# The low parts of the output projections' weights by an accumulating DMA in place of VectorE

## The chip, the cores and the metric

The kernel runs on one core of one Trainium2 chip. The metric is the device time of one execution in microseconds, as the median of several runs. The kernel before takes 1111.75 us (3 runs, 1111.43 to 1113.39).

## The reference

A trunk of two decoder layers over 512 tokens of width 1024, all in float32. Layer a mixes by causal pooling, layer b by stick-breaking attention against a shared K/V; both have four memory attention heads beside the mixer, an output projection and a SwiGLU feed-forward part. The change concerns the output projections alone (`a_w_out` and `b_w_out` below):

```python
def pool_layer(x, mem, mem_norm, norm_mix, w_in, w_group, scale, w_mem_kv, w_out, norm_ffn, w_gu, w_down):
    ...
    x = x + jnp.concatenate([grouped, mem_out], axis=-1) @ w_out
    return x + swiglu(rmsnorm(x, norm_ffn), w_gu, w_down)

def sb_layer(x, mem, k_sh, v_sh, mem_norm, norm_mix, w_q, w_mem_kv, w_out, norm_ffn, w_gu, w_down):
    ...
    x = x + jnp.concatenate([sb_out, mem_out], axis=-1) @ w_out
    return x + swiglu(rmsnorm(x, norm_ffn), w_gu, w_down)
```

## The kernel before, in words

TensorE multiplies in a reduced float32 form (fp32r), so each operand is split in a high part (the value rounded to fp32r) and a low part (the rest). `mm3` (L252 to L259) forms a product in three matmuls: wh·xh (L257), wh·xl (L258) and wl·xh (L259); the low part of the weight is thus needed by the third.

The weights come in bricks of 128 x 512. `bricks` (L169) walks the list PLAN of all bricks; SyncE (SP) loads two bricks per DMA of 512 KB (L183) into one of NRAW = 4 raw chunks `wr_...`, and `wsplit` (L198) makes of each brick `wh` (a cast by ScalarE, ACT, L209) and `wl` (a subtraction by VectorE, DVE, L210, or L213 and L214 where a gain belongs to the weight). There are 4 buffers of wh and 4 of wl, and `next_brick` makes bricks AHEAD = 2 before the one in use. A brick of an output projection feeds 12 matmuls of TensorE (PE): 4 output tiles, three matmuls each. A raw chunk is free for the next load when both its bricks are split, and a wl buffer when the last third matmul of its brick has read it.

The projections a_out and b_out have 16 bricks each, called here b0 to b15. Their matmuls are woven into the attention heads by two blocks in which the order on PE is written out from a planner's estimates (`chain`, `wait`); elsewhere, and on all other engines, a scheduler orders the instructions. On the way: SP also issues the copies of the keys `kh<-hk` and `kb<-kl` (L518), that the scores `zs` (L589, L590) read; ACT makes the softmax terms of memory attention (`pt`, L571 and L576), transposed by PE (`tp`, L540); GpSimd (POOL) masks (`nb`, `be`, L594 and L596) and adds up squares for the next norm (`ssq`, L270). `evac` adds the projection to the residual stream on DVE (`x`, L742).

Of the kernel before, what the change touches and what calls it, by code (L numbers as in the profile page):

```python
# [11 lines left out]
F32 = mybir.dt.float32  # L12
F32R = mybir.dt.float32r
AF = mybir.ActivationFunctionType
ALU = mybir.AluOpType
# [98 lines left out]
class Net:  # L114
# [50 lines left out]
    def bricks(self):  # L165

        at, chunk = {}, {}
        for name, ks, gains in PLAN:
            w = self.a[name]  # L169
            _, _, cb, cols = w.shape  # L170
            for k in ks:
                i = at.get(name, 0)
                at[name] = i + 1
                c, b = divmod(i, cb)
                if b == 0:
                    t = self.wp.tile([P, cb, cols], F32, tag="wraw", name=f"wr_{name}_{c}", bufs=NRAW)
                    if i == 0 and name == "a_in":
                        for j in range(cb):
                            self.nc.sync.dma_start(t[:, j, :], w[c, :, j, :])
                            if j == 0:  # L180
                                self.first()
                    else:
                        self.nc.sync.dma_start(t, w[c])  # L183
                    chunk[name] = t
                yield name, self.wsplit(chunk[name][:, b, :], k, gains, name == "b_last")

    def next_brick(self, name):

# [6 lines left out]
        assert got == name  # L195
        return parts

    def wsplit(self, w, k, gains=None, stays=False):  # L198

        nc = self.nc  # L200
        cols = w.shape[-1]
        self.chain([("act", cols), ("dve", cols)])
        if stays:
            wh, wl = self.t("xh", F32R), self.t("xl", F32R)
        else:
            wh = self.wp.tile([P, cols], F32R, tag="wh", name="wh", bufs=4)
            wl = self.wp.tile([P, cols], F32R, tag="wl", name="wl", bufs=4)
        if gains is None:
            nc.scalar.copy(wh, w)  # L209
            nc.vector.tensor_tensor(out=wl, in0=w, in1=wh.bitcast(F32), op=ALU.subtract)  # L210
        else:
            for c0, c1, g in gains:
                nc.scalar.activation(wh[:, c0:c1], w[:, c0:c1], AF.Copy, scale=self.gain(g, k))  # L213
                nc.vector.scalar_tensor_tensor(  # L214
                    out=wl[:, c0:c1], in0=w[:, c0:c1], scalar=self.gain(g, k),
                    in1=wh.bitcast(F32)[:, c0:c1], op0=ALU.mult, op1=ALU.subtract)
        return wh, wl
# [792 lines left out]
def _chunks(bricks, cb=2):  # L1010
    b = np.stack(bricks)
    n, p, c = b.shape
    return np.ascontiguousarray(b.reshape(n // cb, cb, p, c).transpose(0, 2, 1, 3))
# [63 lines left out]
```

## Time and profile before

| | |
|---|---|
| median of 3 runs | 1111.75 us |
| the profiled execution | 1111.37 us, of which the span of the profile 1109.7 us |
| PE, PEld busy | 1086.1 us (98%), 912.8 us (82%) |
| DVE, ACT, POOL busy | 677.1 us (61%), 499.8 us (45%), 79.1 us (7%) |
| granted TensorE clock, mean | 0.996 |
| DMA | 117.48 MB, 106 GB/s in the mean; none is issued by POOL |

The times in the rows are microseconds from the span's start. A matmul's own duration is longer than its distance to the next, because matmuls overlap: the distance says what one costs. What stands in brackets at a row's end is how long the engine had been idle ahead of it, and what ended that. The projection a_out lies between 88 and 146 us, b_out between 654 and 737 us.

### The profile page before, as it was taken

To read this page: it belongs to the slowest core of one execution; us is meant where nothing else is said; L and a number is where in the kernel's file an instruction comes from. 1 tells how busy PE (TensorE), PEld (TensorE's weight loads), DVE (VectorE), ACT (ScalarE), POOL (GpSimd) and SP (SyncE) were. 2 spreads that over 40 slices of the span, in tenths; PEclk is the share of its full clock that TensorE was granted. 3 is DMA by queue.
4 is the path that set the end of the run, shared out by engine and by line. 5 is a ranking of instruction groups with operands and counts; after the bars stand their busy time and mean duration, and the time that the engine had idled before them with its cause. 6 is when DMAs were issued, how large, how long until landed. Compare 5 with 4: busy or idle time off the path is not lost.

```text
span 1109.7 us, 14396 instructions
## 1 busy us (share of the span) xinstructions
PE 1086.1 (98%) x5280; PEld 912.8 (82%) x5280; DVE 677.1 (61%) x1118; ACT 499.8 (45%) x913; POOL 79.1 (7%) x126
## 2 busy tenths in 40 slices
PE   9989999999999999999999999999999999999997
PEld 7988888888888888888877887788888888888887
DVE  7987666543454534565579698884563365435574
ACT  7558444332333323344797576553332233323343
POOL 0000120000000000000013143240000000000000
PEclk9999999999999999999999999999999999999999
DMA  7454222322222222323445424122222223222212
GB/s 272 138 175 124 95 90 93 102 96 95 95 95 95 95 97 102 103 96 92 138 133 131 132 84 111 60 93 95 95 96 99 97 100 103 96 95 95 95 57 77
DMA packets 39366, 117.48 MB, mean 106 GB/s; under 512 B 5120, under 2 KB 7168, under 8 KB 39296
## 3 DMA queue, kind: packets, MB, share of 16 engines
q1 hardware_dynamic: 39152, 116.54, 32.5%
q8 instruction: 41, 0.67, 0.2%
q14 instruction: 29, 0.24, 0.1%
q10 hardware_dynamic: 144, 0.03, 0.0%
HBM read 100.83 MB, written 2.10 MB: 93 GB/s over the span
## 4 chain that ended last, share of the span: by engine, by line
PE 53%; issue 40%; DVE 3%; ACT 2%; DMA 1%; POOL 1%; SPq 0%; POOLq 0%; DVEq 0%; ACTq 0%
PE acc L257 15%; PE acc L258 15%; PE acc L259 15%; PE av L629 2%; PE tp L540 1%; DVE wl L214 1%; DVE it L599 1%; DMA wr_a_in<-in_a_in_dram 1%; PE zs L590 0%; DMA kb<-kl 0%; PE last L257 0%; PE zs L589 0%; PE last L258 0%; PE last L259 0%; POOL nb L594 0%
## 5 line engine op out<-in xcount | busy, mean ns | idle before, releaser
L257 PE MATMUL acc<-xh,wh 128*128 128x512 f32 x880 | 342.9, 392 | 2.1 <-DVE mx L567 1.1
L258 PE MATMUL acc<-xl,wh 128*128 128x512 f32 x880 | 342.8, 390 | 0.0
L259 PE MATMUL acc<-xh,wl 128*128 128x512 f32 x880 | 342.1, 390 | 0.0
L257 PEld LDWEIGHTS acc<-xh,wh 128*128 128x128 f32 x880 | 165.2, 188 | 35.4 <-ACT xh L223 1.7
L259 PEld LDWEIGHTS acc<-xh,wl 128*128 128x128 f32 x880 | 165.2, 188 | 34.7
L258 PEld LDWEIGHTS acc<-xl,wh 128*128 128x128 f32 x880 | 165.4, 188 | 32.9 <-DVE xl L224 0.2
L214 DVE SCALAR_TENSOR_TENSOR wl<-wr_a_gu,gains,wh 128x512 fp32r<-128x512 f32 x88 | 67.0, 762 | 110.8 <-ACT wh L213 110.8
L214 DVE SCALAR_TENSOR_TENSOR wl<-wr_b_gu,gains,wh 128x512 fp32r<-128x512 f32 x88 | 66.9, 762 | 105.5 <-ACT wh L213 105.5
L213 ACT ACTIVATE wh<-wr_a_gu,gains 128x512 fp32r<-128x512 f32 x88 | 63.6, 724 | 139.0 <-PE acc L258 111.8
L257 PE MATMUL acc<-hh,wh 128*128 128x512 f32 x320 | 124.5, 389 | 0.0
L258 PE MATMUL acc<-hl,wh 128*128 128x512 f32 x320 | 124.5, 389 | 0.0
L259 PE MATMUL acc<-hh,wl 128*128 128x512 f32 x320 | 124.3, 389 | 0.0
L213 ACT ACTIVATE wh<-wr_b_gu,gains 128x512 fp32r<-128x512 f32 x88 | 63.6, 724 | 133.4 <-PE acc L258 104.0
L258 PEld LDWEIGHTS acc<-hl,wh 128*128 128x128 f32 x320 | 60.1, 188 | 12.5
L259 PEld LDWEIGHTS acc<-hh,wl 128*128 128x128 f32 x320 | 60.1, 188 | 12.5
L257 PEld LDWEIGHTS acc<-hh,wh 128*128 128x128 f32 x320 | 60.1, 188 | 12.4
L210 DVE TENSOR_TENSOR wl<-wr_a_down,wh 128x512 fp32r<-128x512 f32 x44 | 30.4, 690 | 60.1 <-ACT wh L209 49.9
L286 POOL TENSOR_TENSOR rs<-var,mhalf 128x4 f32<-128x4 f32 (+1 forms) x7 | 6.6, 942 | 758.3 <-DVE var L284 758.3
L209 ACT CAST wh<-wr_a_down 128x512 fp32r<-128x512 f32 x44 | 27.4, 622 | 72.6 <-PE acc L258 67.9
L210 DVE TENSOR_TENSOR wl<-wr_b_down,wh 128x512 fp32r<-128x512 f32 x36 | 24.8, 690 | 49.1 <-ACT wh L209 41.0
L257 PE MATMUL acc<-mixh,wh 128*128 128x512 f32 x128 | 51.0, 399 | 0.3 <-DVE x L742 0.3
L259 PE MATMUL acc<-mixh,wl 128*128 128x512 f32 x128 | 50.2, 392 | 0.0
(199 smaller groups left out, 1696.7 us busy)
## 6 DMA issues: line engine op xcount, KB each, us to landing
wr_a_gu<-in_a_gu_dram SPq DMA_DIRECT2D x44, 512.0 KB, 3.4
wr_b_gu<-in_b_gu_dram SPq DMA_DIRECT2D x44, 512.0 KB, 3.4
wr_a_down<-in_a_down_dram SPq DMA_DIRECT2D x22, 512.0 KB, 3.4
wr_b_qkv<-in_b_qkv_dram SPq DMA_DIRECT2D x20, 512.0 KB, 3.6
wr_b_down<-in_b_down_dram SPq DMA_DIRECT2D x18, 512.0 KB, 3.4
wr_a_out<-in_a_out_dram SPq DMA_DIRECT2D x8, 512.0 KB, 3.5
wr_b_out<-in_b_out_dram SPq DMA_DIRECT2D x8, 512.0 KB, 3.4
wr_a_in<-in_a_in_dram SPq DMA_DIRECT2D x7, 512.0 KB, 4.2
```

What stands on the lines that cost most here:

```text
L209: nc.scalar.copy(wh, w)
L210: nc.vector.tensor_tensor(out=wl, in0=w, in1=wh.bitcast(F32), op=ALU.subtract)
L213: nc.scalar.activation(wh[:, c0:c1], w[:, c0:c1], AF.Copy, scale=self.gain(g, k))
L214: nc.vector.scalar_tensor_tensor(out=wl[:, c0:c1], in0=w[:, c0:c1], scalar=self.gain(g, k), in1=wh.bitcast(F32)[:, c0:c1], op0=ALU.mult, o ...
L257: mm(ps, wh, xh, start=first, stop=False)
L258: mm(ps, wh, xl, start=False, stop=False)
L259: mm(ps, wl, xh, start=False, stop=last)
L286: nc.gpsimd.tensor_tensor(out=rs, in0=var, in1=self.mhalf[:, :nt], op=ALU.pow)
L540: nc.tensor.transpose(tp[:, i * P:(i + 1) * P], blk, self.ident)
L599: nc.vector.tensor_tensor_scan(out=it[:, :end][:, ::-1], data0=nb[:, :end][:, ::-1], data1=nb[:, :end][:, ::-1], initial=1.0, op0=ALU.mult ...
L629: self.nc.tensor.matmul(to, vv, part, start=ia == 0 and i == 0, stop=ia == nu - 1 and i == len(parts) - 1)
```

## The change

For the bricks of a_out and b_out the low part is no longer a DVE subtraction. ACT writes the negated high part into wl (an added pass over 128 x 512), and POOL issues a DMA of 256 KB that adds the raw weight to what stands in wl. All other bricks are as before.

```diff
@@ bricks @@
-                yield name, self.wsplit(chunk[name][:, b, :], k, gains, name == "b_last")
+                yield name, self.wsplit(chunk[name][:, b, :], k, gains, name == "b_last", name.endswith("_out"))
@@ wsplit @@
-    def wsplit(self, w, k, gains=None, stays=False):
+    def wsplit(self, w, k, gains=None, stays=False, dma=False):
...
         if gains is None:
             nc.scalar.copy(wh, w)
-            nc.vector.tensor_tensor(out=wl, in0=w, in1=wh.bitcast(F32), op=ALU.subtract)
+            if dma:
+                nc.scalar.activation(wl, wh.bitcast(F32), AF.Copy, scale=-1.0)
+                nc.gpsimd.dma_start(wl.bitcast(F32), w, accum_op=ALU.add)
+            else:
+                nc.vector.tensor_tensor(out=wl, in0=w, in1=wh.bitcast(F32), op=ALU.subtract)
```

The lines below the edit move down by four (L540 becomes L544, and so on); the added pass is L211, the DMA L212. The planner's list of work is the same, so the order on PE inside the two blocks is the same. DVE loses 32 instructions, ACT gains 32, POOL 32 DMAs. Where the scheduler decides, it moves some. Three places follow.

ACT at the start of a_out, where the heads of memory attention end. `wh_1174` is the high part of b0 and `wr_a_out_0`, `_1` the raw chunks of b0 to b3. Before:

```order
L551 COPY tb_1138<-av_1117 64x512
L223 CAST ath_1146<-tp_1141 128x512
L571 ACTIVATE pt_1120,sm_1129<-zm_1121,mx_1126,sp_324 128x256 x2
L209 CAST wh_1206<-wr_a_out_0_1172 128x512
L223 CAST ath_1155<-tp_1150 128x512
L814 ACTIVATE mixh_1181<-accg_1159,gains_67 128x512
L576 ACTIVATE pt_1120<-pt_1120,sm_1129 128x256 x2
L209 CAST wh_1233<-wr_a_out_1_1231 128x512
L814 ACTIVATE mixh_1213<-accg_1160,gains_67 128x512
L209 CAST wh_1297<-wr_a_out_1_1231 128x512
L571 ACTIVATE pt_1188,sm_1197<-zm_1189,mx_1194,sp_324 128x256 x2
L814 ACTIVATE mixh_1220<-accg_1161,gains_67 128x512
```

And now, from the negation of b1 on (`pt_1189`, `mixh_1215` and `mixh_1222` were `pt_1188`, `mixh_1213` and `mixh_1220`):

```order
L211 ACTIVATE wl_1208<-wh_1207 128x512
L580 ACTIVATE pt_1120<-pt_1120,sm_1129 128x256 x2
L575 ACTIVATE pt_1189,sm_1198<-zm_1190,mx_1195,sp_324 128x256 x2
L209 CAST wh_1300<-wr_a_out_1_1233 128x512
L818 ACTIVATE mixh_1215<-accg_1160,gains_67 128x512
L211 ACTIVATE wl_1236<-wh_1235 128x512
L555 COPY tb_1245<-av_1226 64x512
L580 ACTIVATE pt_1189<-pt_1189,sm_1198 128x256 x2
L575 ACTIVATE pt_1252,sm_1261<-zm_1253,mx_1258,sp_324 128x256 x2
L211 ACTIVATE wl_1301<-wh_1300 128x512
L818 ACTIVATE mixh_1222<-accg_1161,gains_67 128x512
```

The negations of b1 and b2 (`wl_1208`, `wl_1236`) stand ahead of the normalisation of `pt_1189`, as does that of b0, which stands right behind the cast of `ath_1146`; one `mixh` pass has moved behind it.

SP where b_out begins: `wr_b_out_4` (buffer `wr_b_out_6854` here) goes into the raw chunk of b0 and b1 of b_out. Before:

```order
L183 DMA wr_b_out_6830<-in_b_out_dram 128x1024 [waits DMAHW2_49,DVE_49]
L518 DMA kh<-hk 64x512 [waits DMAHW3_49,Activation_49]
L518 DMA kh<-hk 64x512 [waits DMAHW4_49]
L518 DMA kh<-hk 64x512 [waits DMAHW5_49]
L518 DMA kh<-hk 64x512 [waits DMAHW6_49]
L518 DMA kb<-kl 64x512 [waits DMAHW7_49,DVE_49]
L518 DMA kb<-kl 64x512 [waits DMAHW0_49]
```

And now:

```order
L183 DMA wr_b_out_6854<-in_b_out_dram 128x1024 [waits DMASW1_49,DMAHW2_49,DMASW0_49,Activation_49]
L522 DMA kh<-hk 64x512 [waits DMAHW3_49,Activation_49]
L522 DMA kh<-hk 64x512 [waits DMAHW4_49]
L522 DMA kh<-hk 64x512 [waits DMAHW5_49]
L522 DMA kb<-kl 64x512 [waits DMAHW6_49,DVE_49]
L522 DMA kb<-kl 64x512 [waits DMAHW7_49]
L522 DMA kh<-hk 64x512 [waits DMAHW0_49]
```

The load waited for DVE and now waits for the two accumulating DMAs of b0 and b1 (DMASW0 and DMASW1); the copies of the keys stand behind it, and one `kh` has changed places with the first two `kb`. The DMA of b1 stands on POOL behind the select of `be` that ran at 660.25.

POOL at the end of a_out. Before, all rows of a_out:

```order
L286 TENSOR_TENSOR rs_473<-var_471,mhalf_76 128x2
L270 TENSOR_TENSOR ssq_1452<-ssq_1452,sq_1467 128x512
L270 TENSOR_TENSOR ssq_1452<-ssq_1452,sq_1483 128x512
L270 TENSOR_TENSOR ssq_1452<-ssq_1452,sq_1499 128x512
L270 TENSOR_TENSOR ssq_1452<-ssq_1452,sq_1631 128x512
```

Now, from the tenth DMA on (`wr_a_out_5` holds b10 and b11):

```order
L212 DMA wl_1448<-wr_a_out_4_1437 128x512
L274 TENSOR_TENSOR ssq_1462<-ssq_1462,sq_1477 128x512
L212 DMA wl_1519<-wr_a_out_5_1516 128x512
L212 DMA wl_1536<-wr_a_out_5_1516 128x512
L274 TENSOR_TENSOR ssq_1462<-ssq_1462,sq_1493 128x512
L274 TENSOR_TENSOR ssq_1462<-ssq_1462,sq_1509 128x512
L212 DMA wl_1555<-wr_a_out_6_1552 128x512
L212 DMA wl_1572<-wr_a_out_6_1552 128x512
L212 DMA wl_1591<-wr_a_out_7_1588 128x512
L212 DMA wl_1608<-wr_a_out_7_1588 128x512
L274 TENSOR_TENSOR ssq_1462<-ssq_1462,sq_1647 128x512
```

The DMAs of b10 and b11 stand behind the first addition of squares, those of b12 to b15 behind the third. At the end of both projections PE has also moved: behind the first two matmuls of b15 stand matmuls of the feed-forward part (18 in layer b, 6 in layer a) ahead of the first that reads the wl of b15.

## Rows read from the trace of the kernel before

**Rows 1.** The page's first part: busy time of each engine over the span.
```profile
PE 1086.1 (98%) x5280; PEld 912.8 (82%) x5280; DVE 677.1 (61%) x1118; ACT 499.8 (45%) x913; POOL 79.1 (7%) x126
```

**Rows 2.** Windows: from:to, length, busy us of each engine, PE clock, DMA share, GB/s.
```profile
95.00:105.00 10.00, 9.12 (x47) 7.38 (x47) 7.75 (x17) 9.95 (x26) 0.00 (x0) 1.00 0.31 106
...
680.00:695.00 15.00, 15.00 (x77) 12.29 (x76) 14.73 (x25) 10.65 (x25) 7.88 (x15) 1.00 0.10 36
```

**Rows 3.** Waits of PE over the whole span: us in total, times, longest.
```profile
PE tp L540 <- ACT pt L576: 3.0, 3, 1.2
PE zs L590 <- DMA kb<-kl: 2.8, 2, 1.8
```

**Rows 4.** Lines L209 and L210: duration in ns (minimum/median/maximum), first and last start.
```profile
L209 ACT CAST wh<-wr_a_out x16: 602/622/638, 88.6 to 134.4; 128x512 fp32r<-128x512 f32 x16
...
L210 DVE TENSOR_TENSOR wl<-wr_a_out,wh x16: 679/691/1772, 89.3 to 135.1; 128x512 fp32r<-128x512 f32 x16
```

**Rows 5.** DMA issues: times issued, KB each, median us from issue to landing.
```profile
wr_a_out<-in_a_out_dram SPq DMA_DIRECT2D x8, 512.0 KB, 3.5
...
kh<-hk SPq DMA_DIRECT2D x24, 128.0 KB, 2.4
...
xin<-in_x_dram SPq DMA_DIRECT2D x8, 256.0 KB, 6.8
```

**Rows 6.** Timeline of POOL: start, us, instruction, times, idle before.
```profile
123.69 1.68 POOL L270 TENSOR_TENSOR ssq<-ssq,sq 128x512 f32<-128x512 f32 x1 [86.36 <-ACT sq L266]
...
660.25 0.93 POOL L596 TENSOR_SCALAR_AFFINE_SELECT be<-be 128x128 f32<-128x128 f32 x1
...
699.44 2.54 POOL L594 TENSOR_SCALAR_AFFINE_SELECT nb<-nb 128x128 f32<-128x128 f32 x1 [0.38 <-ACT nb L592]
701.93 0.29 POOL L596 TENSOR_SCALAR_AFFINE_SELECT be<-be 128x128 f32<-128x128 f32 x1
```

**Rows 7.** Timeline of ACT in a_out.
```profile
90.83 0.59 ACT L223 CAST ath<-tp 128x512 fp32r<-128x512 f32 x1
91.31 0.57 ACT L571 ACTIVATE pt<-zm,mx,sp 128x256 f32<-128x256 f32 x1
...
98.69 0.91 ACT L576 ACTIVATE pt<-pt,sm 128x256 f32<-128x256 f32 x2
...
123.52 1.12 ACT L209 CAST wh<-wr_a_out 128x512 fp32r<-128x512 f32 x2
```

**Rows 8.** Timeline of PE in a_out.
```profile
95.73 0.39 PE L259 MATMUL acc<-mixh,wl 128*128 128x512 f32 x1
...
99.25 0.72 PE L540 MATMUL tp<-ident,pt 128*128 128x128 f32 x2 [0.81 <-ACT pt L576]
...
129.41 0.39 PE L259 MATMUL acc<-mixh,wl 128*128 128x512 f32 x1
129.64 0.39 PE L257 MATMUL acc<-mixh,wh 128*128 128x512 f32 x1
```

**Rows 9.** Timeline of SP where b_out begins: the issues themselves.
```profile
659.98 0.33 SPq L183 DMA_DIRECT2D wr_b_out<-in_b_out_dram  x1
664.28 2.39 SPq L518 DMA_DIRECT2D kh<-hk  x4
667.01 2.39 SPq L518 DMA_DIRECT2D kb<-kl  x4
```

**Rows 10.** Timeline of PE where b_out begins, and at 729.
```profile
669.90 0.33 PE L590 MATMUL zs<-kb,qs 128*128 128x128 f32 x1 [1.81 <-DMA kb<-kl]
...
729.22 0.39 PE L259 MATMUL acc<-mixh,wl 128*128 128x512 f32 x1
729.90 0.50 PE L257 MATMUL acc<-mixh,wh 128*128 128x512 f32 x1 [0.29 <-DVE x L742]
```

**Rows 11.** Windows around the wait of 668: columns as in rows 2.
```profile
671.10:674.50 3.40, 3.40 (x17) 3.20 (x16) 1.68 (x4) 1.17 (x2) 0.21 (x1) 0.51 0.55 125
```

**Rows 12.** Timeline of DVE at the end of b_out.
```profile
727.45 1.79 DVE L210 TENSOR_TENSOR wl<-wr_b_out,wh 128x512 fp32r<-128x512 f32 x1
```

## The prediction

> **What bounds the kernel now.** I read the busy times first: PE is busy for 98% of the span, DVE for 61%, POOL for 7% [rows 1]. Work taken from DVE is therefore worth something only where PE waits for DVE. The windows tell where that could be [rows 2]: between 680 and 695 DVE is busy for 14.73 of 15 us, but PE for all 15.00, so a faster DVE brings nothing there; between 95 and 105 it is ACT that is full (9.95 of 10), and PE misses 0.88. The list of waits names what ends these gaps [rows 3]: ACT's `pt`, and the copy of the keys `kb`; neither names a low part of a weight. The timelines give the places: 0.81 ahead of `tp` at 99.25 [rows 8], 1.81 ahead of `zs` at 669.90, and 0.29 ahead of the projection's first matmul at 729.90 [rows 10]. Of the three only the last is behind DVE's `wl`: that subtraction took 1.79 at 727.45 where its median is 0.69 [rows 4, 12], the residual add came after it, and PE waited for the add.
>
> **What is removed and added.** 32 subtractions of 0.69 leave DVE: 22 us of an engine with 433 us to spare. ACT gets 32 passes of 128 x 512. I price one as the cast of the same size: 0.62 by itself [rows 4], 0.50 when it follows another, since two casts back to back took 1.12 [rows 7]; 16 to 20 us in all. PE's matmuls are the same in number. So the engine sums decide nothing; what decides is how long the new low part takes to be there, and who stands behind it. Call L the time from POOL's issue of the accumulating DMA to wl landed. Before, the step between wh and the use was a subtraction of 0.69; now it is a pass on ACT and L.
>
> **The size of L.** No row shows an accumulate, nor any DMA that POOL issues. The nearest rows: a plain copy of 128 KB takes 2.4 from issue to landing, a load of 512 KB 3.5, the slowest landing of a 256 KB tile (at the kernel's start) is 6.8 [rows 5]. The accumulate moves 256 KB but reads two operands, 512 KB; by bytes it is nearest to the 3.5. POOL must also write the list of transfers itself; the nearest rows for a pass of POOL are 0.93 (a select) and 1.68 (an add) [rows 6], 1.3 in the middle. I take L = 3.5 + 1.3 = 4.8, with 2.4 and 6.8 as ends. The lower end could only undercut a plain copy of half the bytes, which I exclude.
>
> The copy of 128 KB here takes 2.4 and the load of 512 KB 3.5 [rows 5]. The Trainium skill (DMA: Bandwidth & Descriptors, section "Anatomy of one DMA — SWDGE (gpsimd) path") gives about 2.0 us plus the bytes over 436 KB per us for a DMA issued by GpSimd, and both rows lie close to that line. By it 256 KB would take an estimated 2.6, and the sum below would be that of the first rival.
>
> **First term: the start of a_out.** The first matmul that reads a low part of a_out is at 95.73 [rows 8]. The negation of b0 now stands behind the cast of `ath` (90.83), where a `pt` pass began at 91.31; it ends at 91.31 + 0.62 = 91.93 [rows 7]. The budget is 95.73 - 91.93 = 3.80, and with L = 4.8 PE waits 1.0. There is a second path: ACT is full here, three negations come ahead of the `pt` normalisation at 98.69 that ended the wait of 0.81, and one pass leaves: net two of 0.50, another 1.0 on that wait. The two overlap, because a PE that is 1.0 late anyway asks for `tp` 1.0 later. The term is the larger: max(1.0, L - 3.80) = +1.0. Below zero it can't go, since nothing leaves ACT here. Bricks b1 to b9 cost nothing at that L; the cover is the two bricks that are prepared ahead, 5.4 us of PE, since a brick is 12 matmuls and they start 0.23 apart (129.41, 129.64) [rows 8].
>
> **Second term: b10.** At the end of a_out the DMAs stand on POOL between additions of squares. The casts of b10 and b11 start at 123.52 and 124.02, the negation of b10 at 124.52 and ends at 125.14 [rows 7]; POOL is in its addition until 123.69 + 1.68 = 125.37 [rows 6]; the low part is wanted at 129.41 [rows 8]. Budget 4.04, cost L - 4.04 = +0.76. From then on PE is later by that much and the bricks behind it, with the same two bricks of cover less the passes of ACT, are inside it. Without the additions in the way the budget would be 4.27, so the queue itself costs 0.23. The last brick of each layer is covered by the matmuls of the feed-forward part that now stand ahead of it (6 x 0.23 = 1.4 in a, 18 x 0.23 = 4.1 in b); without this cover b15 of layer b, issued only behind two additions of 1.68 on POOL, would cost up to 3.4.
>
> **Third term: SP at the start of b_out.** The load of the fifth raw chunk must wait until both DMAs on the first chunk have read it, and the copies of the keys are queued behind it on SP. The DMA of b1 leaves POOL behind the select that ends at 660.25 + 0.93 = 661.18 [rows 6]; it lands at 665.98; the load's issue takes 0.33, so the first `kh` goes at 666.31 in place of 664.28 [rows 9]. With 0.60 for each issue (2.39 for four) three `kh` and the first `kb` are through at 668.71, and the second `kb` issues there. Before, it issued at 667.01 + 0.60 = 667.61, and `zs` ran 2.29 later, at 669.90 [rows 10]. Now it runs at 671.00: the wait of 1.81 grows by 1.10, or L - 3.70. Waiting behind `zs` on PE is all the rest of b_out. The selects of POOL, which stand behind its DMAs, are the other thing that moves; PE is full from 680 on [rows 2], so I cost them at nothing; the cover is the projection's own matmuls, woven between the heads, and if it is gone each DMA's 1.3 on POOL is a price that the first heads would pay.
>
> **What is gained.** Without the subtraction at 727.45 the residual add comes as soon as PE is done with its tile, and the matmul at 729.90 follows 0.23 after that of 729.22, as others do: 0.45 less [rows 10, 12]. What is late next is nothing on that chain.
>
> **The sum.** 1.0 + 0.76 + 1.10 - 0.45 = +2.4 in the profiled execution of 1111.37 us (span 1109.7, 1.67 around it). That execution is 0.38 below the median of the runs, 1111.75, and the difference is put onto the median: 1114.2. The bounds: at L = 2.4 only the ACT path is left, 1.0 - 0.45 = +0.55; at L = 6.8 it is 3.0 + 2.76 + 3.10 - 0.45 = +8.4.
>
> **Rivals.** *The DMA lands in time.* L at most 3.7: +0.55, 1112.3, no measurable change (a measurement of this kernel tells 0.2%, 2.2 us). For it speak the plain copies at 2.4, against it the doubled reads. The sum passes 2.2 at L = 4.7, so this is the rival on the other side of the line: not slower for every L below that.
>
> *The clock follows the wait.* Right behind the wait of 1.81 the granted clock was 0.51 for 3.4 us [rows 11], the level of 1.2 GHz, which cost 1.7. The wait at 99.25, now 0.81 with no drop behind it in a window at 1.00 [rows 2], would become 1.8 if the ACT path and not b0 sets it. A second drop makes 1115.9.
>
> *POOL is held up while it writes.* A select of the same shape took 2.54 at 699.44 and 0.29 at 701.93, beside DVE work [rows 6]. If a DMA's list is stretched by that difference, 2.25, L is 7.05 and the sum 3.25 + 3.01 + 3.35 - 0.45 = +9.2: 1120.9. Against it: DVE is emptier now. The Trainium skill (SBUF — State Buffer, section "Who interferes with whom") has a DVE instruction with two inputs contend only with a GpSimd instruction that reads SBUF; by that rule the writing of the list would be spared, and L would stay near 4.8.
>
> *DVE's relief reaches the keys.* With L under 2.8 SP isn't held, `kl` can come up to a subtraction (0.69) earlier, and if the shorter wait also spares the clock drop (1.7), the sum is 0 (ACT absorbed) - 0.45 - 0.69 - 1.7 = -2.8: 1108.9. It needs three things at once.
>
> **Chances.** The forecast case (L from 4.1 to 5.6, its own range 1112.7 to 1116.6) has 0.40, in time 0.29, the clock 0.11, POOL held up 0.13, the keys 0.07. Of the forecast case some two thirds lie above the line of 2.2: slower 0.27 + 0.11 + 0.13 = 0.51, same 0.29 + 0.13 = 0.42, faster 0.07. The range leaves out the far part of POOL's rival and most of the keys': 1111.2 to 1119.5.
>
> **What would show it.** The rows of the DMA on POOL give L itself. Right if PE's list has waits on it near 96 and 130, a longer wait for `kb` near 670, and none for the add at 729. Wrong if PE between 95 and 146 waits no more than before (L small), if PE waits show between 680 and 725 (POOL's selects late), or if more than 4 us of waits stand at other bricks, which would mean that two bricks ahead do not cover L.

## The result, and the profile after

The changed kernel takes 1121.45 us (median of 4 runs, 1120.59 to 1122.42) against 1111.64 before (4 runs): a ratio of 1.0089, with a 95% interval from 1.0077 to 1.0101. It is slower by 9.8 us, where +2.4 was forecast and 1119.5 was the upper end. The profiled execution has a span of 1118.9 us, 9.2 more than before. The engine sums moved about as worked out, against [rows 1]: DVE lost 19.5 us, ACT gained 19.0, POOL 26.0, and PE's busy time grew by 3.8 us at the same number of matmuls, of which 2.5 is time at a low clock (table below). The first part of the page:

```profile
PE 1089.9 (97%) x5280; PEld 913.9 (82%) x5280; DVE 657.6 (59%) x1086; ACT 518.8 (46%) x945; POOL 105.1 (9%) x158
```

The DMA issues of the page (times issued, KB each, median us from issue to landing) give the size that no row of before had. L is 3.7 and 3.2 in the median, not 4.8, and POOL is busy for 0.87 per DMA. The copies of the keys have become slower, 3.0 and 2.8 where they took 2.4 [rows 5] and 2.5:

```profile
wl<-wr_a_out POOLq DMA_DIRECT2D x16, 256.0 KB, 3.7
...
wl<-wr_b_out POOLq DMA_DIRECT2D x16, 256.0 KB, 3.2
...
kh<-hk SPq DMA_DIRECT2D x24, 128.0 KB, 3.0
kb<-kl SPq DMA_DIRECT2D x24, 128.0 KB, 2.8
```

So the transfer is quicker than forecast and the kernel slower. PE's list of waits (us in total, times, longest) says where to look. Against [rows 3], `tp` has grown by 0.9, and three lines are new: `kh`, `mixl`, and the low part itself, which has only 1.0 of it:

```profile
PE tp L544 <- ACT pt L580: 3.9, 3, 1.7
...
PE zs L593 <- DMA kh<-hk: 2.4, 1, 2.4
PE zs L594 <- DMA kb<-kl: 2.4, 2, 1.3
PE acc L261 <- DVE mixl L819: 2.1, 1, 2.1
...
PE acc L263 <- DMA wl<-wr_a_out: 1.0, 1, 1.0
```

**Lining up the matmuls.** PE's order is the same in both kernels through most of the two projections, so each matmul of one execution can be set against the same matmul of the other, and the difference of their starts read as a running delay. This is the table that it gives (us from each span's start):

| PE instruction | before | after | delay | what came since the line above |
|---|---|---|---|---|
| `av`, before the first wait | 95.96 | 95.91 | -0.05 | |
| `tp` | 99.25 | 100.10 | +0.85 | wait for `pt`, 1.70 in place of 0.81: +0.9 |
| a_out, the next tile | 100.52 | 103.61 | +3.09 | wait for `mixl`, 2.08: +2.2 |
| a_out | 103.27 | 108.89 | +5.62 | half clock: +2.5 |
| a_out, b12's low part used | 134.85 | 141.66 | +6.81 | wait for the DMA, 1.00: +1.2 |
| `zs` of the keys before b_out | 631.42 | 638.79 | +7.37 | +0.6, in many small pieces |
| `zs<-kb` | 669.90 | 679.46 | +9.56 | `kh` 2.44 and `kb` 1.33 in place of 1.81: +2.2 |
| b_out, behind the add | 729.90 | 738.97 | +9.07 | the wait of 0.29 is gone: -0.5 |

**The start of a_out.** On ACT (timeline: start, us, instruction) the negation of b2 stands at 98.37 ahead of the `pt` normalisation, which comes at 99.54 where it came at 98.69 [rows 7]; the third `mixh` pass is now behind the negation of b3, at 102.09. DVE makes `mixl` of it at 102.80, and PE's next matmul waits for that until 103.61. It then takes 0.79 and its followers 0.63, where such a matmul takes 0.39:

```profile
98.37 0.66 ACT L211 ACTIVATE wl<-wh 128x512 fp32r<-128x512 f32 x1
99.05 0.58 ACT L555 COPY tb<-av 64x512 f32<-64x512 f32 x1
99.54 0.91 ACT L580 ACTIVATE pt<-pt,sm 128x256 f32<-128x256 f32 x2
...
101.57 0.62 ACT L211 ACTIVATE wl<-wh 128x512 fp32r<-128x512 f32 x1
102.09 0.68 ACT L818 ACTIVATE mixh<-accg,gains 128x512 fp32r<-128x512 f32 x1
```

The same pass before, the `mixl` that DVE makes of it, and PE's matmul, which waited for neither:

```profile
97.46 0.72 ACT L814 ACTIVATE mixh<-accg,gains 128x512 fp32r<-128x512 f32 x1
```

```profile
98.94 0.74 DVE L815 SCALAR_TENSOR_TENSOR mixl<-accg,gains,mixh 128x512 fp32r<-128x512 f32 x1
```

```profile
100.52 0.39 PE L257 MATMUL acc<-mixh,wh 128*128 128x512 f32 x1
```

DVE's row now, and below it three of PE's:

```profile
102.80 0.75 DVE L819 SCALAR_TENSOR_TENSOR mixl<-accg,gains,mixh 128x512 fp32r<-128x512 f32 x1 [0.93 <-ACT mixh L818]
```

```profile
100.10 0.73 PE L544 MATMUL tp<-ident,pt 128*128 128x128 f32 x2 [1.70 <-ACT pt L580]
...
103.61 0.79 PE L261 MATMUL acc<-mixh,wh 128*128 128x512 f32 x1 [2.08 <-DVE mixl L819]
104.20 0.63 PE L262 MATMUL acc<-mixl,wh 128*128 128x512 f32 x1
```

The windows (columns as in rows 2) show the two costs apart: from 95 to 105 PE is busy for 6.15 where it was 9.12 [rows 2], and from 105 to 115 it is full, but at a granted clock of 0.80: part of that stretch ran at the level of 1.2 GHz, where before it was 1.00 throughout.

```profile
95.00:105.00 10.00, 6.15 (x28) 4.45 (x27) 5.08 (x12) 9.95 (x26) 2.62 (x3) 0.86 0.61 128
105.00:115.00 10.00, 10.00 (x42) 8.09 (x40) 1.45 (x3) 5.58 (x11) 2.37 (x3) 0.80 0.46 109
```

And the second of these stretches before:

```profile
105.00:115.00 10.00, 10.00 (x50) 8.26 (x49) 4.71 (x8) 4.51 (x9) 0.00 (x0) 1.00 0.22 69
```

**The end of a_out.** The DMA of b12 leaves POOL at 135.54, behind the additions of squares, and PE wants it at 140.66. That is 5.1 later, more than the usual L; but this one takes 6.1:

```profile
141.66 0.50 PE L263 MATMUL acc<-mixh,wl 128*128 128x512 f32 x1 [1.00 <-DMA wl<-wr_a_out]
```

The view of line L212 in a window around a single DMA (issues with durations in ns, then the time to landing) shows two sizes: 3.2 for the one at 111.63, with no load and no other accumulating DMA under way, and 6.1 for the one at 135.54, right beside the load that SP issues at 135.88. A load is let go as soon as the accumulating DMAs on its raw chunk have landed (the later of b10's and b11's at 135.7), so the two kinds meet again and again. Of the 16 DMAs of a_out the five that left within 0.7 of a load (99.32, 114.37, 122.95, 135.54 and 136.3) took 4.5 to 6.6. A sixth slow one, 5.3 from 138.88, left while two others were still under way. The other ten took 3.2 to 4.0.

```profile
L212 POOL DMA_DIRECT2D wl<-wr_a_out x1: 872/872/872, 111.6 to 111.6; - x1
...
DMA to landing us min/median/max: 3.2/3.2/3.2
```

```profile
L212 POOL DMA_DIRECT2D wl<-wr_a_out x1: 879/879/879, 135.5 to 135.5; - x1
...
DMA to landing us min/median/max: 6.1/6.1/6.1
```

And SP's issue of the load in its timeline:

```profile
135.88 0.33 SPq L183 DMA_DIRECT2D wr_a_gu<-in_a_gu_dram  x1
```

The Trainium skill's line for a DMA issued by GpSimd (DMA: Bandwidth & Descriptors, "Anatomy of one DMA — SWDGE (gpsimd) path") makes an estimated 2.6 of 256 KB. An accumulate alone took 3.2 here, so that line is nearer than the 4.8 of the forecast, and it does not tell of the 6.1.

**The start of b_out.** SP's load of the fifth raw chunk went out at 672.2, and the copies of the keys follow it at 672.59. Taken back by the delay of 7.37 that is 665.22, 0.94 later than in [rows 9]. Each copy then lands in 4.2 to 4.6 us; the copies of before landed in 2.2 to 2.3 there. PE waits 2.44 for `kh`, which it did not wait for at all before, and 1.33 for `kb`. The late issue alone would have cost little: before, the second `kb` was issued at 667.51 and `zs` ran 2.39 later; now it is issued at 675.05, which plus 2.39 is 677.44, or 670.07 by the time of before, an estimated 0.2 more than 669.90. The other 2.0 are the slow landing. SP's timeline first:

```profile
658.26 14.24 SPq L183 DMA_DIRECT2D wr_b_out<-in_b_out_dram  x2
672.59 1.75 SPq L522 DMA_DIRECT2D kh<-hk  x3
674.55 1.10 SPq L522 DMA_DIRECT2D kb<-kl  x2
```

The landing of the copies issued between 672 and 676 (line L522), that of the six of before (line L518, 664 to 668), and PE's two waits now:

```profile
DMA to landing us min/median/max: 4.2/4.4/4.6
```

```profile
DMA to landing us min/median/max: 2.2/2.3/2.3
```

```profile
677.83 0.30 PE L593 MATMUL zs<-kh,qs 128*128 128x128 f32 x1 [2.44 <-DMA kh<-hk]
679.46 0.45 PE L594 MATMUL zs<-kb,qs 128*128 128x128 f32 x1 [1.33 <-DMA kb<-kl]
```

### The profile page after: what moved, and what is told of

Same layout as the page of the kernel before. It is cut to its first block, busy times and chain, and to the rows that moved or that the text cites. A ratio compares the mean times of both kernels' runs of the same rounds, so it can differ in the third digit from the quotient of the medians.

```text
span 1118.9 us, 14469 instructions
## 1 busy us (share of the span) xinstructions
PE 1089.9 (97%) x5280; PEld 913.9 (82%) x5280; DVE 657.6 (59%) x1086; ACT 518.8 (46%) x945; POOL 105.1 (9%) x158
## 4 chain that ended last, share of the span: by engine, by line
PE 87%; DVE 4%; ACT 3%; issue 2%; DMA 2%; POOL 1%; SPq 0%; POOLq 0%; DVEq 0%; ACTq 0%
PE acc L261 27%; PE acc L263 27%; PE acc L262 26%; PE av L633 2%; PE tp L544 1%; DMA kb<-kl 1%; DVE wl L218 1%; PE zs L594 1%; DMA wl<-wr_a_out 1%; DMA wr_a_in<-in_a_in_dram 1%; ACT pt L575 1%; ACT pt L580 0%; PE zs L593 0%; DVE it L603 0%; PE ps_ss L285 0%
## 5 line engine op out<-in xcount | busy, mean ns | idle before, releaser
L209 ACT CAST wh<-wr_a_down 128x512 fp32r<-128x512 f32 x44 | 27.4, 624 | 72.5 <-PE acc L262 67.8
```

## The experiments

The theory that these rows suggest: three places and not the DMAs in sum. ACT's passes and their order at the start of a_out (theory A; C says that the moved `mixh` pass is the larger half, D that any added pass weighs the same), the late b12, and the load that is let go beside the keys. The rival (B) is that the accumulating DMAs cost something wherever they stand. All diffs are against the changed kernel, except where the kernel before is named. The times of the kernel before are those of the same chip and job.

**Without any accumulating DMA.** The negation stays, DVE adds.

```diff
-                nc.gpsimd.dma_start(wl.bitcast(F32), w, accum_op=ALU.add)
+                nc.vector.tensor_tensor(out=wl, in0=w, in1=wl.bitcast(F32), op=ALU.add)
```

> The negation stays on ScalarE, but VectorE adds the raw weight to it: no accumulating DMA at all. Theory A (the loss is mostly ScalarE's: the added passes push the pt normalisation and one mixh pass of the first heads back, and the clock drops behind the waits): the start of a_out keeps its waits of about 1.7 and 2.1 us and its half clock, +5.7 us, and the later losses (the last bricks of a_out, the keys in b_out) go: about 1117.3. Theory B (the loss is the DMA's: its landing, its list on GpSimd, its traffic): 1111.6 to 1112.6, only the 1.0 of ScalarE's passes left.

Measured 1117.03 against 1111.15, ratio 1.0051 (1.0036 to 1.0066): +5.9. PE's timeline has both waits at the same two places, and the window the low clock, with POOL idle. The wait for `kb` is 2.40 here, 0.6 longer than before, which theory A did not expect. This run alone shows that more than half of the loss needs no DMA.

```profile
99.97 0.86 PE L544 MATMUL tp<-ident,pt 128*128 128x128 f32 x2 [1.80 <-ACT pt L580]
...
103.51 0.79 PE L261 MATMUL acc<-mixh,wh 128*128 128x512 f32 x1 [1.39 <-DVE mixl L819]
```

Its window from 95 to 105, columns as in rows 2:

```profile
95.00:105.00 10.00, 6.74 (x28) 4.87 (x27) 6.91 (x15) 9.95 (x27) 0.00 (x0) 0.77 0.27 89
```

**The DMA without ACT's pass.** The reverse: DVE negates.

```diff
-                nc.scalar.activation(wl, wh.bitcast(F32), AF.Copy, scale=-1.0)
+                nc.vector.tensor_scalar(out=wl, in0=wh.bitcast(F32), scalar1=-1.0, scalar2=None, op0=ALU.mult)
```

> The negation is made by VectorE, the accumulating DMA stays: ScalarE has the work of the kernel before. Theory A: the waits at the start of a_out are again at most 0.9 us with no clock drop; what stays is the late wl near the end of a_out (1.2 to 1.4) and the keys in b_out (2.2, less 0.4): about 1114.8. Theory B: as the changed kernel, 1120 to 1122.

Measured 1114.63 against 1111.15, ratio 1.0031 (1.0019 to 1.0043): +3.5. The wait for `pt` is back to 0.82, that for `mixl` is gone; 0.52 for a low part at 130 and 2.64 for the keys (`kh` 1.30, `kb` 1.34) are there. The 5.9 of the run before and this 3.5 add up to 9.4 of the 9.8.

**One layer.**

```diff
-name.endswith("_out"))
+name == "a_out")
```

> Only a_out's 16 bricks by DMA, b_out as before. Both kernels' matmuls lined up say that the changed kernel is 7.3 us late when layer a's output projection is done, and 9.2 at the end. If the layers add up: 1111.6 + 7.3 = 1118.9. If the loss in layer b comes from what was already late (a shifted clock window), more than 1120.

Measured 1118.13 against 1111.15, ratio 1.0064 (1.0049 to 1.0079): +7.0. That is close to the 7.3 that the lined-up matmuls gave to layer a, and leaves 2.8 for layer b. No run changed all of b_out alone; its two parts below gave +4.0 and +0.7, each with the clock's share in it.

**26 of the 32 DMAs.**

```diff
-name.endswith("_out"))
+(name == "a_out" and i >= 4) or (name == "b_out" and i >= 2))
```

> By DMA are only the bricks b4 to b15 of a_out and b2 to b15 of b_out (26 of 32); the others as before. Theory A (three places, not the sum of DMAs): the start of a_out is as before, SP's load at the start of b_out doesn't wait for a DMA, so only the late wl near the end of a_out stays, +0.8 to +1.4: about 1112.7. Theory B: 26/32 of +9.8, about 1119.6.

Measured 1111.46 against 1111.15, ratio 1.0003 (0.9994 to 1.0013). Theory B, which wanted 1119.6, falls: the loss needs the other six bricks, and these 26 DMAs together cost nothing that can be measured. One late low part is left in PE's timeline, against the 0.45 gained at the add:

```profile
136.05 0.50 PE L263 MATMUL acc<-mixh,wl 128*128 128x512 f32 x1 [0.93 <-DMA wl<-wr_a_out]
```

**All but b0 of a_out.** This leaves three added passes at the start, with `mixh` where it was.

```diff
-name.endswith("_out"))
+name.endswith("_out") and not (name == "a_out" and i == 0))
```

> As the changed kernel, but b0 of a_out is split by VectorE as before: one negation less at the start of a_out, and the scheduler then leaves the third mixh pass ahead of the pt normalisation, where it was. Theory C (that moved mixh pass is the second wait, 2.1, and the two waits close together bring the half clock, 2.5): what is left is 1.0 for two added passes ahead of tp, 1.4 near the end of a_out, 2.2 less 0.4 in b_out: 1111.2 + 4.2 = 1115.4. Theory D (the added passes alone fill ScalarE and bring both waits, whatever the order): three quarters of the loss at the start stay, about 1118.5.

Measured 1118.15 (1115.65 to 1118.46) against 1110.52, ratio 1.0061 (1.0047 to 1.0074): +7.6 by the medians, not the +4.2 of C. Its trace speaks for C: at the start of a_out there is one wait, 1.95 for `pt`, none for `mixl`, and the clock is full there; but the clock is low in two other places, between 580 and 600 and, as in the kernel before, between 660 and 680. Time and trace do not agree, and this run by itself decided nothing; the further executions below say more.

**Two DMAs.** Only b0 and b1 of b_out.

```diff
-name.endswith("_out"))
+name == "b_out" and i < 2)
```

> Only two of the 32 bricks go by DMA: b0 and b1 of b_out. Theory A: SP's load of the fifth raw chunk waits for these two and then runs beside the copies of the keys; all of layer b's loss comes from them: +2.2, about 1113.4. A loss shared by all DMAs would give 2/32 of 9.8, about 1111.8.

Measured 1114.51 against 1110.52, ratio 1.0036 (1.0023 to 1.0050): +4.0, more than expected. The wait for the keys is that of the changed kernel (`kh` 2.24, `kb` 1.37; the copies land in 4.0 to 4.7, the two accumulating DMAs in 3.2 and 3.3), and adds 2.1 in the lined-up matmuls. The rest of this execution's delay, which was the longest of the four, is older than the change's first instruction: 2.9 at 88 us, 1.5 of it from a low clock between 60 and 80. So two DMAs suffice for the wait of layer b; that the rest of the +4.0 is the clock's is not shown by this trace (see the mean clocks below).

```profile
673.59 0.30 PE L593 MATMUL zs<-kh,qs 128*128 128x128 f32 x1 [2.24 <-DMA kh<-hk]
675.25 0.30 PE L594 MATMUL zs<-kb,qs 128*128 128x128 f32 x1 [1.37 <-DMA kb<-kl]
```

**Traffic ahead of the keys.** In the kernel before, two DMAs of 256 KB into the output.

```diff
         nc.vector.tensor_tensor(out=kl, in0=kf, in1=hk.bitcast(F32), op=ALU.subtract)
         out = []
+        if extra:
+            for n in (0, 4):
+                nc.sync.dma_start(self.out[:, n:n + 4, 0:128], hk.bitcast(F32).rearrange("p (i t) -> p i t", i=4))
...
-                kst[2 * i], kst[2 * i + 1] = net.dup_k(f)
+                kst[2 * i], kst[2 * i + 1] = net.dup_k(f, i == 4)
```

> The kernel before, no accumulating DMA; SP issues two DMAs of 256 KB (the keys' high part into the output, which is overwritten at the end) right ahead of the copies of the last keys, so that 512 KB are in flight with them, as the late load is in the changed kernel. Their two issues cost SP about 1, and the copies of the low part wait for VectorE until 667.0 anyway. If the traffic is what makes the keys late: copies land in 4 to 5 us in place of 2.3, +1.5 to +2.5, about 1113. If it is only SP's queue that held them: no more than +0.5, about 1111.5.

Measured 1111.62 against 1110.52, ratio 1.0006 (0.9996 to 1.0016). The `kh` copies right behind it land in 2.4 to 2.5, those of `kb` in 2.2 to 2.3, and the waits are 0.40 and 1.16, together less than the 1.81 of before. This traffic hardly slows them.

**Loads ahead of the keys.** As above, but from HBM.

```diff
+        if extra:
+            for j in range(2):
+                t = self.t("sg")
+                nc.scalar.copy(t[:, :1], hk.bitcast(F32)[:, :1])
+                nc.sync.dma_start(t, self.a["b_out"][0, :, j, :])
```

> The kernel before, with two loads of 256 KB from HBM on SP between the first copy of the last keys and the next (into tiles that nothing reads). Its question is that of the run with the two DMAs into the output, which hardly slowed the keys: there the bytes left SBUF, here they come from HBM, as those of the late chunk do. If a load ahead in SP's queue is what makes the copies land late: 4 to 5 us in place of 2.3 and a longer wait for the keys, +1.5 to +2.5, 1112.7. If not: at most +0.7, 1111.5.

Measured 1111.99 against 1111.24, ratio 1.0006 (0.9995 to 1.0016). The copy behind the two loads lands in 3.2, not 2.3, and PE waits 1.24 for `kh` and 0.79 for `kb`: 2.03 in place of 1.81. The `kb` copies, issued 1.1 and 1.6 later, land in 2.6 and 2.7. So a load ahead does slow a copy, by up to 0.9 here, but not by the 2.1 of the changed kernel (4.4 against 2.3 in the median). That the copies of the changed kernel ran beside one load of 512 KB is seen; why that costs more than two of 256 KB stays open.

**b2 to b15 of b_out.**

```diff
-name.endswith("_out"))
+name == "b_out" and i >= 2)
```

> Only b2 to b15 of b_out by DMA, nothing else changed. Theory A: none of the three bad places is touched, and the 0.45 at the add near the end of b_out is gained: 1110.7 (1110.2 to 1111.3). If the DMAs cost something of their own wherever they are: 14/32 of 9.8 is +4.3, 1115.4.

Measured 1111.25 against 1110.52, ratio 1.0008 (0.9999 to 1.0017). 14 DMAs, no +4.3; but the expected gain of 0.45 does not show in the time either. In the trace it does: PE's wait for the add is gone.

**The first four bricks of a_out.**

```diff
-name.endswith("_out"))
+name == "a_out" and i < 4)
```

> Only the first four bricks of a_out by DMA: ScalarE has the four negations at the start of a_out, the third mixh pass stands behind the pt normalisation, and nothing else differs. Theory C: all of the loss at the start of a_out is here, 1.0 + 2.2 in two waits and 1.7 to 2.5 in the clock behind them: +5.3, 1116.0 (1115 to 1117). If the loss at the start was the DMAs' doing in sum, 4/32 of 9.8: 1111.9.

Measured 1116.79 against 1111.24, ratio 1.0049 (1.0036 to 1.0063): +5.5 from 4 of 32 DMAs. PE's timeline has both waits of the changed kernel, to 0.01. Both stand 1.4 later than there, since this execution had a low clock between 60 and 80 too (0.91), ahead of anything that was changed; behind the second wait the lined-up delay is 3.1 without these 1.4.

```profile
101.47 0.73 PE L544 MATMUL tp<-ident,pt 128*128 128x128 f32 x2 [1.70 <-ACT pt L580]
104.97 0.74 PE L261 MATMUL acc<-mixh,wh 128*128 128x512 f32 x1 [2.07 <-DVE mixl L819]
```

**Three of these four.**

```diff
-name.endswith("_out"))
+name == "a_out" and 1 <= i < 4)
```

> Only b1, b2 and b3 of a_out by DMA: three negations, but the third mixh pass stays ahead of the pt normalisation. Theory C: one wait of about 1.9 at tp in place of 0.8, +1.1, about 1111.9 (up to 1113.6 where the clock drops behind it). Theory D (each added pass weighs the same): three quarters of the run with four bricks, +4.

Measured 1114.58 (1112.08 to 1116.76) against 1111.24, ratio 1.0027 (1.0016 to 1.0038): +3.0, between C and D. In the trace there is one wait of 1.98 and a delay of 1.2 behind it, as C had it, and the next tile is not waited for; the times spread over 4.7 us.

```profile
99.33 0.69 ACT L818 ACTIVATE mixh<-accg,gains 128x512 fp32r<-128x512 f32 x1
```

```profile
100.47 0.72 PE L544 MATMUL tp<-ident,pt 128*128 128x128 f32 x2 [1.98 <-ACT pt L580]
...
101.73 0.40 PE L261 MATMUL acc<-mixh,wh 128*128 128x512 f32 x1
```

The delay of 3.1 with four bricks and of 1.2 with three differ by 1.9. The fourth negation, some 0.5 of ACT by the prediction's price, is too small for that by itself. But the two come together in every run here: no run has four negations with the pass in front, or three with it moved.

**Squares on DVE.** The run with 26 DMAs, and:

```diff
-                        net.stat_add(st, x[m], nc.gpsimd)
+                        net.stat_add(st, x[m], nc.vector if l == "a" else nc.gpsimd)
```

> As the run with b4 to b15 of a_out and b2 to b15 of b_out, but VectorE adds up the squares of a_out, so that no DMA of a_out stands behind an addition on GpSimd. If the late wl near the end of a_out (0.93) came from GpSimd's order: the wait is gone, and the time is 0.9 lower than that run's, 1110.3, unless VectorE, full there, is late itself. If it came from landing beside the loads (6 us in place of 3.2): a wait of 0.5 or more stays.

Measured 1111.75 against 1111.24, ratio 1.0005 (0.9995 to 1.0015): in the time no difference from the run with 26 DMAs. In the trace the wait of 0.93 is gone, though b13's DMA still took 6.2 to land. That of b12 left at 128.84 and landed in 3.2, where it had left at 130.00 and taken 6.0; PE wanted it at 135.12 in the run with 26. Leaving at 128.84 it would have been there in time with 6.0 as well (134.84), and leaving at 130.00 with 3.2. So, by this sum, the late b12 needs both: the place behind POOL's additions and the slow landing. The run changed both at once.

**Four more executions.** Two of the run with b1 to b3, one of the run with all but b0, one of the kernel before, each traced.

> A second look at the run with b1, b2 and b3 of a_out. Its times lie between 1112.1 and 1116.8, its one profile has the wait of 1.98 at tp and no drop of the clock there. If the drop behind that wait comes in some executions and not in others: a window from 95 to 115 with a granted clock under 0.9 in some of these looks, and then a time some 2 higher than in the looks without. If every look has the clock at 1.00 there, the spread comes from elsewhere.

> A third look, with the same question: granted clock between 95 and 115, and the time beside it.

> The kernel before again: its one profile has the half clock once, behind the wait for the keys at 670. If that drop is by chance, another look has it elsewhere or not at all, and its time is lower or higher by about 1.7 for each drop.

> A second look at the run in which b0 of a_out alone is split by VectorE (times 1115.65 to 1118.5, wait of 1.95 at tp, no drop there in its first profile). If the clock drops behind it in some executions: a window from 95 to 115 under 0.9 here or not, and a time above or below 1117 with it.

With b1 to b3: 1111.72 and 1112.42, with waits of 1.97 and 1.96 at `tp` and no window of 20 us with a clock under 0.985, against 1110.54 for the kernel before beside them: +1.2 and +1.9, near C's size, as far as single executions go. With all but b0: a wait of 1.97, and this time the clock fell behind it, where it had not behind 1.95 in the first trace. The windows of the two programs, first the one with b1 to b3:

```profile
95.00:105.00 10.00, 7.96 (x42) 6.45 (x41) 5.05 (x13) 9.95 (x26) 2.78 (x3) 1.00 0.58 120
```

And the one with all but b0, second trace:

```profile
95.00:105.00 10.00, 7.96 (x36) 6.28 (x36) 5.31 (x12) 9.95 (x26) 2.81 (x3) 0.84 0.64 128
```

PE is busy for 7.96 in both, and gets 42 matmul records done in the one and 36 in the other. And the kernel before, traced again, has its wait of 1.83 for the keys without the drop of [rows 11], at 1110.81.

So behind a wait of about 2 us the clock falls in some executions and not in others: here, at 670, and at 67 (behind 1.77 and 1.89 in the runs with the first four and with two bricks, not behind 1.73 in the kernel before). At 590 it falls in three of these runs behind two shorter waits, 0.60 to 0.76 and 0.90 to 0.91, that the kernel before has too. The kernel before itself spreads by 4.5 us (1109.41 to 1113.94 in one job).

The mean granted clock of every timed execution is on record, and 0.001 of it is an estimated 1.1 us of the span. Executions of one job with the same mean can be set side by side (medians, with the number of executions):

| run | mean clock | its time | the kernel before | difference | its waits |
|---|---|---|---|---|---|
| first four bricks | 0.994 | 1116.96 (2) | 1113.54 (3) | 3.4 | 3.1 |
| all but b0 | 0.994 | 1118.15 (2) | 1113.56 (2) | 4.6 | 4.2 by C |
| two DMAs | 0.996 | 1114.17 (2) | 1111.71 (7) | 2.5 | 2.1 |
| b1 to b3 | 0.996 | 1113.35 (5) | 1112.04 (13) | 1.3 | 1.2 |
| b1 to b3 | 0.997 | 1112.31 (2) | 1109.82 (6) | 2.5 | 1.2 |

So the clock makes up most of the difference between the traces and the times, at the resolution that the rounded means allow; for b1 to b3 a part stays open.

What is shown is that with `mixh` ahead of the `pt` normalisation the second wait is absent in all five traces of these two programs, and that with `mixh` moved it is there in all four that have it so (the changed kernel, a_out alone, no DMA, the first four bricks: 1.39 to 2.08), each time with a low clock behind it, where only one of the five others has one there.

No kernel of these beats the one before; the best two (26 DMAs; b2 to b15 of b_out) can't be told from it.

## Why the prediction was wrong

*What bounds the kernel, and what is removed:* right. The work taken from DVE was worth 0.5, the wait at the add, as forecast (0.45).

*The size of L:* too high for a DMA that runs alone. 3.2 there and 3.2 to 3.7 in the median against 4.8, since POOL needs 0.87 and not 1.3, and what is left of 3.2 without it, 2.3, is a plain copy's time [rows 5] and not that of a load of the same bytes. By the sum's own rule, max(1.0, L - 3.80) and so on, an L of 3.5 would have given +0.55, the first rival. So the right L would have put the forecast further off: the mistake that counts is in the terms of the sum.

*First term, the start of a_out:* the step that failed. "Three negations come ahead of the `pt` normalisation ... and one pass leaves: net two of 0.50." The wait at `tp` did grow by 0.9, by ACT and not by the DMA (b0's landed at 95.5, and its matmul ran at 95.58), as that path said. But the pass that leaves was booked as relief, and nobody asked who waits for it. It was the third `mixh`; behind it stand `mixl` on DVE and PE's next matmuls. That is a wait of 2.08, +2.2, and the run with the first four bricks has it with nothing changed behind them. That it is the moved pass rather than the fourth negation is read from the rows (PE behind `mixl`, `mixl` behind `mixh`, `mixh` 4.6 later than before) and from the runs with three, not from a run that moves the pass alone. The order rows had it in plain sight. None of the signs of being wrong that the prediction named covers it.

*The clock:* the rival was named (0.11, "a wait of 1.8") and came, with 2.5 and not 1.7, behind two waits close together. It should have had a larger chance, because the sum itself made the wait as long as the one behind which the clock had already fallen. It is not certain even so: behind a single wait of 1.95 to 1.98 it fell in one trace of five.

*Second term, b10:* the mechanism (a DMA queued behind POOL's additions) was right, the brick and the price were not: b12, with +1.2 where 0.76 stood, and its landing took 6.1 beside a load, which the sum did not have.

*Third term, SP at the start of b_out:* right that the copies of the keys stand behind the load, and on when: the first copy went 0.94 later, where the term's rule gives 0.83 for the 3.6 that b1's DMA took (2.03 for its 4.8). By that rule, L - 3.70, the term would have been nothing; 2.2 came where 1.10 stood, and nearly all of it is another thing, the slow landing of the copies. The load was counted as 0.33 of issue on SP; that its 512 KB land with the copies was not counted at all. Two DMAs alone reproduce the wait.

*The rival of POOL held up while it writes*, whose 1120.9 is near to the measured time, is wrong all the same: a DMA occupies POOL for 0.86 to 1.20, and 26 of them cost nothing that can be measured.

In sum, 0.9 + 2.2 + 2.5 + 1.2 + 0.6 + 2.2 - 0.5 = 9.1 of the 9.2 in the span. Of these 0.9, 1.2 and -0.5 were in the forecast in some form; that 1.10 stood at the place of the last 2.2 is in good part luck, since its cause was another.

## What to carry to other kernels

When a scheduler moves an instruction to make room for an added one, follow the moved one too: its consumer's wait is a term of its own, and it can be larger than the added work. A transfer that is released later has two prices, what is queued behind its issue and what shares its way while it lands. Moving work from an engine with time to spare to one that is full just where the bound engine waits was a loss here, whatever the sums over the span say.

## What the runs showed of the hardware

An accumulating DMA of 256 KB from SBUF into SBUF, issued by POOL, landed 3.2 us after its issue when no load and no other such DMA was under way, and 4.5 to 6.6 when it left within 0.7 of a load of 512 KB; POOL was busy with it for 0.87, at most 1.20. A copy of 128 KB took 2.2 to 2.3 at the start of b_out in the kernel before, 3.2 right behind two loads of 256 KB, 4.0 to 4.7 behind one of 512 KB, and 2.2 to 2.5 behind two DMAs of 256 KB that wrote to HBM. The same program had the granted clock fall behind a wait of 1.97 in one execution and not behind 1.95 in another, and the kernel before had it fall behind 1.81 and not behind 1.83.
